# The small products of a triangular solver, given a higher priority in the schedule of a decoder layer

## The chip, the core and the metric

The kernel runs on one core of a Trainium2 chip. The metric is the device time of one execution in microseconds (us); the kernel before takes 859.18 us (median of three runs, 858.14 to 862.75).

## What is computed

One decoder layer over 512 positions of width 1024. A combined input projection feeds a pooling mixer and a gated DeltaNet mixer of 8 heads; the two are gated, added, projected, normalised, and go through a feed-forward block and an embedding gate. The change touches one step of the DeltaNet mixer alone, the unit lower triangular solve inside each chunk of 64 positions:

```python
m = jnp.where(strict, jnp.einsum('bnhid,bnhjd->bnhij', kb, k) * decay, 0.0)
a = m + jnp.eye(CHUNK, dtype=m.dtype)
rhs = jnp.concatenate([v * beta[..., None], kb * jnp.exp(gc)[..., None]], axis=-1)
sol = lax.linalg.triangular_solve(a, rhs, left_side=True, lower=True, unit_diagonal=True)
...
def step(state, inp):                      # the scan over the chunks
    v_new = u_n - jnp.einsum('bhcd,bhde->bhce', w_n, state)
    o = jnp.einsum('bhcd,bhde->bhce', qg_n, state) + jnp.einsum('bhij,bhje->bhie', attn_n, v_new)
    state = state * jnp.exp(gl_n)[..., None, None] + jnp.einsum('bhcd,bhce->bhde', kg_n, v_new)
```

## The kernel before

The large projections (`gemm_tile`, lines 66 to 68) are done as three products in the fp32r type, each with a 128x128 stationary tile and 512 columns. The small work of the mixer (transposes, the products of the scan, the solver) is in plain fp32; such a product shows as two records of TensorE in the trace.

The heads go in four pairs. For each pair the program has `front` (projections of k, q and v, convolution, the products k k^T and q k^T), then the `scan` of the pair before (lines 509 to 583: eight steps in four blocks of 128 positions, whose products are on lines 542, 543, 552, 558 and 559, and the transposes on line 580), then `solve` of the pair itself. After the last pair come the pooling branch, the last `scan`, the gate projections z, gb and ga, the output projection (wo), and a third stage (up and down projections, from line 827) whose instructions are kept in program order.

`solve` (lines 431 to 507) inverts eight 128x128 blocks per pair. VectorE first inverts the 16x16 diagonal blocks (lines 440 to 453); then the inverse is doubled to 32, 64 and 128 by two groups of products each:

- p16, line 461, and q16, line 468: 32 products each on 32x32 tiles
- p32, line 483, and q32, lines 491 and 493: 16 and 24 products on 32x32 tiles
- p64, line 502, and q64, line 506: 8 products each on 64x64 tiles

Between two groups ScalarE or VectorE copies the result out of PSUM (lines 463, 469 and 470, 486, 496 and 497, 503, 507), and the next group reads that copy. A group is called a burst below. There are six for a pair and 24 in all.

The order on each engine is not written out for these two stages. A scheduler runs the program in a simulated time: whenever an engine is free there, it takes from the instructions that are ready the one of highest priority, and by default that is the one that stands first in the program. So `scan` of the pair before stands ahead of `solve`, and the next pair's `front` stands behind it. The order so found is fixed in the instruction streams; on the chip each engine works through its stream in that order and waits on semaphores. Weight slabs are prepared with a priority raised by 300 (line 56).

Of the kernel before, what the change touches and what calls it, by code (L numbers as in the profile page):

```python
# [33 lines left out]
def layer(tc, x, p, ln_in_g, ln_in_b, w_in, pool_w, pool_scale, conv_w, a_log, dt_bias, o_norm_w,  # L34
          w_out, ln1_g, ln1_b, w_up, w_down, ple_gate_w, ple_proj_w, ln2_g, ln2_b, out):
    nc = tc.nc
    V, A, G, T = nc.vector, nc.scalar, nc.gpsimd, nc.tensor
# [107 lines left out]
    for t in range(NT):  # L145
        xt = mxp.tile([P, DM], F32, tag="big", name=f"x_{t}")
# [62 lines left out]
    for t in range(NT):  # L209
# [7 lines left out]
        a, b = xts[t][:, 0:cut], xts[t][:, cut:1024]  # L217
# [123 lines left out]
    x64, p64 = xp64[0:64], xp64[64:128]  # L341
# [89 lines left out]
    def solve(pr, n, yfull):  # L431

        U8 = 2 * NT
        w = lambda tag, shape, bufs=1: tp1.tile(list(shape), F32, tag=tag, bufs=bufs, name=f"{tag}_{pr}")
        n32 = w("p16", (P, U8, 32))
        for q in range(4):
            r = slice(32 * q, 32 * q + 32)
            A.copy(n32[r], n[r, :, r])
        b16 = w("b16", (P, U8, 16))
        V.tensor_scalar(out=b16, in0=n32[:, :, 0:16], scalar1=lowm, scalar2=None, op0=MULT)  # L440
        V.scalar_tensor_tensor(out=b16, in0=n32[:, :, 16:32], scalar=highm, in1=b16, op0=MULT, op1=ADD)
        ya = w("ya", (P, U8, 16))
        V.tensor_copy(ya, eye16.unsqueeze(1).to_broadcast([P, U8, 16]))
        for k in range(15):
            m = 15 - k
            sh = w("sh", (P, U8, 16), 2)
            V.stream_shuffle(out=sh[:, :, :m], in_=b16[:, :, k + 1:], mask=[k] * 16 + [16 + k] * 16)
            V.tensor_tensor(out=sh[:, :, :m], in0=sh[:, :, :m],
                            in1=ya[:, :, k:k + 1].to_broadcast([P, U8, m]), op=MULT)
            V.tensor_tensor(out=ya[:, :, k + 1:], in0=ya[:, :, k + 1:], in1=sh[:, :, :m], op=ADD)  # L450
        y = w("yc", (P, U8, 32))
        V.tensor_scalar(out=y[:, :, 0:16], in0=ya, scalar1=lowm, scalar2=None, op0=MULT)
        V.tensor_scalar(out=y[:, :, 16:32], in0=ya, scalar1=highm, scalar2=None, op0=MULT)
        xt = w("xc", (P, U8, 32))
        V.transpose(out=xt, in_=y)

        pp = pp1.tile([P, U8, 32], F32, tag="sp", name=f"ps_p16_{pr}")
        for u in range(U8):
            for q in range(4):
                r = slice(32 * q, 32 * q + 32)  # L460
                T.matmul(pp[r, u, :], n[r, u, r], xt[r, u, :], start=True, stop=True)
        p16 = w("p16", (P, U8, 32))
        A.copy(p16, pp)
        pq = pp1.tile([P, U8, 16], F32, tag="sq", name=f"ps_q16_{pr}")
        for u in range(U8):
            for q in range(4):
                r = slice(32 * q, 32 * q + 32)
                T.matmul(pq[r, u, :], p16[r, u, :], y[r, u, 16:32], start=True, stop=True)
        V.scalar_tensor_tensor(out=y[:, :, 16:32], in0=pq, scalar=lowm, in1=y[:, :, 16:32], op0=MULT, op1=ADD)
        V.transpose(out=xt, in_=y)  # L470
        for q in range(4):
            r = slice(32 * q, 32 * q + 32)
            A.copy(yfull[r, :, r], y[r])
        for q in range(2):
            r = slice(32 * q, 32 * q + 32)
            A.copy(x64[r, :, r], xt[r])

        pp = pp1.tile([P, U8, 32], F32, tag="sp", name=f"ps_p32_{pr}")
        p32 = w("p16", (P, U8, 32))
        for q in (0, 2):  # L480
            r, r1 = slice(32 * q, 32 * q + 32), slice(32 * q + 32, 32 * q + 64)
            for u in range(U8):
                T.matmul(pp[r1, u, :], n[r, u, r1], xt[r, u, :], start=True, stop=True)
        for q in (0, 2):
            r1 = slice(32 * q + 32, 32 * q + 64)
            A.copy(p32[r1], pp[r1])
        pq = pp1.tile([P, U8, 32], F32, tag="sq", name=f"ps_q32_{pr}")
        for q in (0, 2):
            r, r1 = slice(32 * q, 32 * q + 32), slice(32 * q + 32, 32 * q + 64)
            for u in range(U8):  # L490
                T.matmul(pq[r, u, :], p32[r1, u, :], y[r1, u, :], start=True, stop=True)
                if q == 0:
                    T.matmul(pq[r1, u, :], y[r1, u, :], p32[r1, u, :], start=True, stop=True)
        for q in (0, 2):
            r, r1 = slice(32 * q, 32 * q + 32), slice(32 * q + 32, 32 * q + 64)
            A.copy(yfull[r, :, r1], pq[r])
        A.copy(x64[32:64, :, 0:32], pq[32:64])

        a, b = slice(0, 64), slice(64, 128)
        pp = pp1.tile([P, U8, 64], F32, tag="sp", name=f"ps_p64_{pr}")  # L500
        for u in range(U8):
            T.matmul(pp[b, u, :], n[a, u, b], x64[:, u, :], start=True, stop=True)
        A.copy(p64, pp[b])
        pq = pp1.tile([P, U8, 64], F32, tag="sq", name=f"ps_q64_{pr}")
        for u in range(U8):
            T.matmul(pq[a, u, :], p64[:, u, :], yfull[b, u, b], start=True, stop=True)
        A.copy(yfull[a, :, b], pq[a])

    def scan(heads, yfull, kq, kg, vs, sm, last=False):
# [90 lines left out]
    def lazy(pr):  # L600
        got = {"k": wk0} if pr == 0 else {}

        class Groups:
            def __getitem__(self, n):
                if n not in got:
                    with tc.issue_after(vec_last.ins), tc.issue_after(act_last.ins):
                        got[n] = wslab({"k": C_K, "q": C_Q, "v": C_V}[n] + 256 * pr, f"{n}{pr}")
                return got[n]
        return Groups()

    prev = None
    for pr in range(NH // 2):
        heads, npr, yfull, kq, kg, vs, sm = front(pr, lazy(pr))
        if prev is not None:
            scan(*prev)
        solve(pr, npr, yfull)
        prev = (heads, yfull, kq, kg, vs, sm)
# [7 lines left out]
    for s in range(2):  # L625
        gr = wslab(C_POOL + 256 * s, f"pool{s}")
        for m in range(2):
# [4 lines left out]
            u = tpa.tile([P, SEQ], F32, tag="acc", bufs=2, name=f"u_{g}")  # L632
# [11 lines left out]
            n = win - 1  # L644
# [224 lines left out]
    def fetch(c, name, i, half):  # L869
        raw = wide(f"{name}_{c}").rearrange("p (j n) -> p j n", j=2)  # L870
        oS.dma_start(out=raw, in_=quarter(c, i, half))
        return raw
# [100 lines left out]
    x, z, y, b22 = fetch(0, "x", 0, 0), fetch(0, "z", 1, 0), None, None  # L973
    oS.dma_start(out=gain1, in_=ln1_g[0].partition_broadcast(P))
    oS.dma_start(out=off1, in_=ln1_b[0].partition_broadcast(P))
    y, b22 = fetch(0, "y", 0, 1), fetch(0, "w", 1, 1)
# [8 lines left out]
    for c in range(NC):  # L985
# [44 lines left out]
        if not lst:  # L1030
# [11 lines left out]
            x, z, y, b22 = nxt + [fetch(c + 1, "y", 0, 1), fetch(c + 1, "w", 1, 1)]  # L1042
# [16 lines left out]
    u = tp3.tile([P, 2, SEQ], F32, tag="r2", bufs=2, name="u")  # L1059
# [111 lines left out]
```

## Time and profile before

| | us |
|---|---|
| median of three runs | 859.18 |
| lowest, highest | 858.14, 862.75 |
| the profiled execution | 858.59 |
| its span, first to last instruction | 856.9 |
| TensorE busy | 838.3 |
| VectorE busy | 612.6 |
| ScalarE busy | 407.8 |

PE is TensorE's matmul, PEld its weight load, DVE is VectorE, ACT is ScalarE. The profiled execution takes 1.7 us more than its span, which lies around the first and the last instruction. In a timeline the first number of a line is its start, the second the time from there to the end of the last record on that line. Matmuls are pipelined and their ends are modelled, so lines overlap; the pace is read from start to start.

### The profile page before, as it was taken

The page shows a single profiled execution, that of the slowest core. Times are in us where ns is not written, and L with a number is a line of the kernel's source. Part 1 is how long each engine was busy: PE and PEld are TensorE (multiplying, and loading weights), DVE is VectorE, ACT ScalarE, POOL GpSimd, SP SyncE. Part 2 cuts the span into 40 slices and gives each one's busy share as a digit, 9 for nine tenths or more (in the row PEclk, how much of TensorE's full clock was granted, in tenths as well). Part 3 has the DMA queues.
Part 4 walks back from the last instruction along what each step waited for, and adds up shares of the span by engine and source line. Part 5 has one row for each costly group of instructions (what it writes and reads, how often), then busy time and mean ns, then how long its engine had stood idle before and what let it go on. Part 6 is the DMA issues. An engine that isn't in the chain of part 4 may idle for free.

```text
span 856.9 us, 12524 instructions
## 1 busy us (share of the span) xinstructions
PE 838.3 (98%) x4848; PEld 697.6 (81%) x4848; DVE 612.6 (71%) x1197; ACT 407.8 (48%) x648; POOL 88.1 (10%) x94
## 2 busy tenths in 40 slices
PE   7999999999999999999999999999999999999996
PEld 6787888888888888888889878888888888888785
DVE  7898968759768436469467795848575767667986
ACT  5566455465464534342309544453535453634510
POOL 4061000002001000010000101111111111110000
PEclk9999999999999999999999999999999999999999
DMA  6323322222221322246216757575757576655221
GB/s 203 98 55 94 88 61 69 81 65 59 81 75 32 86 65 80 73 138 212 100 49 208 187 148 172 126 173 138 175 139 183 135 187 146 158 139 123 75 75 49
DMA packets 73229, 98.47 MB, mean 115 GB/s; under 512 B 4553, under 2 KB 48978, under 8 KB 73170
## 3 DMA queue, kind: packets, MB, share of 16 engines
q1 hardware_dynamic: 64384, 80.87, 29.7%
q0 software_dynamic: 8704, 16.78, 12.0%
q8 instruction: 38, 0.62, 0.3%
q14 instruction: 21, 0.17, 0.1%
q10 hardware_dynamic: 82, 0.02, 0.0%
HBM read 95.56 MB, written 2.10 MB: 114 GB/s over the span
## 4 chain that ended last, share of the span: by engine, by line
PE 86%; DVE 7%; ACT 3%; DMA 2%; issue 1%; POOL 0%; DVEq 0%; SPq 0%; ACTq 0%; POOLq 0%
PE ps_up L839 18%; PE ps_pg L839 5%; PE ps_dny L839 5%; PE ps_dnx L839 5%; PE ps_dn L839 4%; PE ps_dnz L839 2%; PE ps_z L68 2%; PE ps_gb L67 2%; PE ps_z L67 2%; PE ps_ga L68 2%; PE ps_gb L68 2%; PE ps_gb L66 2%; PE ps_z L66 2%; PE ps_ga L66 2%; PE ps_ga L67 2%; DVE res L839 1%
## 5 line engine op out<-in xcount | busy, mean ns | idle before, releaser
L839 PE MATMUL ps_up<-act,hi_up 128*128 128x512 f32 x480 | 147.8, 389 | 0.0
L839 PEld LDWEIGHTS ps_up<-act,hi_up 128*128 128x128 f32 x480 | 90.0, 188 | 18.7
L839 PE MATMUL ps_up<-act,lo_up 128*128 128x512 f32 x240 | 93.4, 389 | 0.0
L839 ACT ACTIVATE r<-ps_up 128x512 f32<-128x512 f32 x32 | 19.1, 596 | 101.4 <-PE ps_up L839 99.5
L839 POOL DMA_DIRECT2D x<-in_w_down_dram x24 | 29.0, 1210 | 279.0 <-DVE lo_dn L839 266.6
L839 PEld LDWEIGHTS ps_up<-act,lo_up 128*128 128x128 f32 x240 | 45.0, 188 | 9.3
L839 DVE TENSOR_TENSOR lo_dn<-x,hi_dn 128x1024 fp32r<-128x1024 f32 x32 | 39.0, 1220 | 6.9 <-ACT hi_dn L839 6.9
L839 PE MATMUL ps_dnx<-hi_dn,hid_s 128*128 128x512 f32 x128 | 42.3, 391 | 0.0
L839 ACT CAST hid_s<-r 128x512 fp32r<-128x512 f32 x32 | 18.3, 618 | 46.1 <-DVE r L839 46.1
L839 ACT CAST hi_dn<-x 128x1024 fp32r<-128x1024 f32 x32 | 33.6, 1051 | 12.3 <-PE ps_dn L839 9.0
L839 PE MATMUL ps_pg<-hi_pg,act 128*128 128x512 f32 (+1 forms) x128 | 36.0, 362 | 0.0
L839 DVE TENSOR_TENSOR hid_b<-r,hid_b 128x512 fp32r<-128x512 f32 x16 | 11.1, 692 | 32.0 <-ACT hid_b L839 32.0
L839 DVE TENSOR_TENSOR lo_up<-raw_up,hi_up 128x1024 fp32r<-128x1024 f32 x28 | 33.5, 1218 | 0.0
L839 DVE TENSOR_TENSOR hid_a<-r,hid_a 128x256 fp32r<-128x256 f32 x16 | 6.8, 425 | 35.2 <-ACT hid_a L839 35.2
L839 DVE TENSOR_TENSOR r<-r 128x256 f32<-128x256 f32 x64 | 27.2, 425 | 2.2
L839 DVE TENSOR_TENSOR hid_s<-r,hid_s 128x512 fp32r<-128x512 f32 x32 | 20.7, 688 | 11.1 <-ACT hid_s L839 11.1
L839 ACT CAST hi_up<-raw_up 128x1024 fp32r<-128x1024 f32 x28 | 28.6, 1045 | 0.0
L839 PEld LDWEIGHTS ps_dnx<-hi_dn,hid_s 128*128 128x128 f32 x128 | 23.9, 188 | 5.7 <-DVE hid_s L839 0.4
L839 PEld LDWEIGHTS ps_pg<-hi_pg,act 128*128 128x128 f32 x128 | 23.1, 189 | 3.8
L576 POOL TENSOR_TENSOR rs<-rs,mhalf 128x4 f32<-128x4 f32 x8 | 9.4, 1174 | 162.8 <-DVE rs L575 162.8
L839 PE MATMUL ps_dnx<-lo_dn,hid_s 128*128 128x512 f32 x64 | 24.9, 389 | 0.0
L839 PE MATMUL ps_dnz<-hi_dn,hid_b 128*128 128x512 f32 x64 | 22.4, 391 | 2.1 <-DVE hid_b L839 2.1
(735 smaller groups left out, 2414.1 us busy)
## 6 DMA issues: line engine op xcount, KB each, us to landing
raw_up<-in_w_up_dram SPq DMA_DIRECT2D x32, 512.0 KB, 6.9
x<-in_w_down_dram POOLq DMA_DIRECT2D x24, 512.0 KB, 5.9
raw_wo<-in_w_out_dram SPq DMA_DIRECT2D x8, 512.0 KB, 4.5
x<-in_w_down_dram SPq DMA_DIRECT2D x8, 512.0 KB
z<-in_w_down_dram SPq DMA_DIRECT2D x8, 512.0 KB
y<-in_w_down_dram SPq DMA_DIRECT2D x8, 512.0 KB
w<-in_w_down_dram SPq DMA_DIRECT2D x8, 512.0 KB, 3.6
y<-in_w_down_dram POOLq DMA_DIRECT2D x8, 512.0 KB, 8.8
```

What stands on the lines that cost most here:

```text
L66: T.matmul(ps, wh, ah, start=first, stop=False)
L67: T.matmul(ps, wh, al, start=False, stop=False)
L68: T.matmul(ps, wl, ah, start=False, stop=last)
L576: G.tensor_tensor(out=rs, in0=rs, in1=mhalf.to_broadcast([P, NT]), op=ALU.pow)
L839: return lambda *a, **k: tc.keep_in_program_order(op(*a, **k))
```

## The change

The six groups of matmuls in `solve` are each put into a block `tc.high_priority(offset=1000)`. That raises the priority of these instructions by 1000 places, which is more than the instructions of `scan` and `front` before them, so in the scheduler's choice they stand ahead of anything else that is ready on TensorE. No instruction is added or removed, and none of the copies between the bursts is in such a block.

```diff
         pp = pp1.tile([P, U8, 32], F32, tag="sp", name=f"ps_p16_{pr}")
-        for u in range(U8):
-            for q in range(4):
-                r = slice(32 * q, 32 * q + 32)
-                T.matmul(pp[r, u, :], n[r, u, r], xt[r, u, :], start=True, stop=True)
+        with tc.high_priority(offset=1000):
+            for u in range(U8):
+                for q in range(4):
+                    r = slice(32 * q, 32 * q + 32)
+                    T.matmul(pp[r, u, :], n[r, u, r], xt[r, u, :], start=True, stop=True)
...
         pq = pp1.tile([P, U8, 32], F32, tag="sq", name=f"ps_q32_{pr}")
-        for q in (0, 2):
-            r, r1 = slice(32 * q, 32 * q + 32), slice(32 * q + 32, 32 * q + 64)
-            for u in range(U8):
-                T.matmul(pq[r, u, :], p32[r1, u, :], y[r1, u, :], start=True, stop=True)
-                if q == 0:
-                    T.matmul(pq[r1, u, :], y[r1, u, :], p32[r1, u, :], start=True, stop=True)
+        with tc.high_priority(offset=1000):
+            for q in (0, 2):
+                r, r1 = slice(32 * q, 32 * q + 32), slice(32 * q + 32, 32 * q + 64)
+                for u in range(U8):
+                    T.matmul(pq[r, u, :], p32[r1, u, :], y[r1, u, :], start=True, stop=True)
+                    if q == 0:
+                        T.matmul(pq[r1, u, :], y[r1, u, :], p32[r1, u, :], start=True, stop=True)
...
         pq = pp1.tile([P, U8, 64], F32, tag="sq", name=f"ps_q64_{pr}")
-        for u in range(U8):
-            T.matmul(pq[a, u, :], p64[:, u, :], yfull[b, u, b], start=True, stop=True)
+        with tc.high_priority(offset=1000):
+            for u in range(U8):
+                T.matmul(pq[a, u, :], p64[:, u, :], yfull[b, u, b], start=True, stop=True)
```

q16, p32 and p64 are changed in the same way.

## Rows read from the trace of the kernel before

**Rows 1.** The page: busy time of the engines, and the chain that ended last.
```profile
PE 838.3 (98%) x4848; PEld 697.6 (81%) x4848; DVE 612.6 (71%) x1197; ACT 407.8 (48%) x648; POOL 88.1 (10%) x94
...
PE 86%; DVE 7%; ACT 3%; DMA 2%; issue 1%; POOL 0%; DVEq 0%; SPq 0%; ACTq 0%; POOLq 0%
```

**Rows 2.** Busy time in three stretches: us, PE, PEld, DVE, ACT, POOL, clock, DMA.
```profile
80.00:100.00 20.00, 19.46 (x92) 15.85 (x91) 19.93 (x74) 8.23 (x12) 1.65 (x1) 1.00 0.36 105
100.00:460.00 360.00, 360.00 (x2626) 301.30 (x2625) 244.41 (x594) 164.21 (x303) 15.51 (x13) 1.00 0.28 83
460.00:500.00 40.00, 37.59 (x218) 32.70 (x217) 31.29 (x43) 24.51 (x45) 5.58 (x5) 1.00 0.75 210
```

**Rows 3.** TensorE's longest wait from 400 us on: total, times, longest.
```profile
PE ps_dnz L839 <- DVE hid_b L839: 2.1, 1, 2.1
```

**Rows 4.** TensorE's timeline: the first broken burst, q16 of the second pair.
```profile
168.64 0.61 PE L468 MATMUL ps_q<-yc,p 32*32 32x16 f32 x50
169.18 0.49 PE L558 MATMUL ps_s<-vn,kg 128*128 128x128 f32 x2
169.51 0.39 PE L559 MATMUL ps_s<-vn,E 128*128 128x128 f32 x2
169.82 0.25 PE L468 MATMUL ps_q<-yc,p 32*32 32x16 f32 x8
...
170.65 0.24 PE L468 MATMUL ps_q<-yc,p 32*32 32x16 f32 x6
170.82 0.50 PE L68 MATMUL ps_q<-act,lo_q3a 128*128 128x512 f32 x1
```

**Rows 5.** TensorE's timeline: the last broken burst, q64 of the fourth pair.
```profile
308.75 0.32 PE L506 MATMUL ps_q<-yfull,xp 64*64 64x64 f32 x2
...
311.16 0.50 PE L66 MATMUL ps_gb<-act,hi_gb1a 128*128 128x512 f32 x1
```

**Rows 6.** TensorE's timeline: four products of the scan between projections.
```profile
160.83 0.39 PE L68 MATMUL ps_k<-act,lo_k3a 128*128 128x512 f32 x1
161.06 0.38 PE L542 MATMUL ps_s<-S,kq 128*128 128x128 f32 x2
...
161.87 0.48 PE L66 MATMUL ps_k<-act,hi_k3a 128*128 128x512 f32 x1
162.19 0.39 PE L67 MATMUL ps_k<-act,hi_k3a 128*128 128x512 f32 x1
```

**Rows 7.** TensorE's timeline: two whole bursts of the first pair and what follows them.
```profile
119.25 0.73 PE L468 MATMUL ps_q<-yc,p 32*32 32x16 f32 x64
119.90 0.66 PE L358 MATMUL ps_kt<-ident,kq 128*128 128x128 f32 x4
...
139.38 1.14 PE L502 MATMUL ps_p<-xp,n 64*64 64x64 f32 x16
140.45 0.50 PE L66 MATMUL ps_v<-act,hi_v2b 128*128 128x512 f32 x1
140.79 0.39 PE L67 MATMUL ps_v<-act,hi_v2b 128*128 128x512 f32 x1
```

**Rows 8.** TensorE's timeline: a whole burst with the scan right behind it.
```profile
237.49 0.73 PE L468 MATMUL ps_q<-yc,p 32*32 32x16 f32 x64
238.15 0.49 PE L558 MATMUL ps_s<-vn,kg 128*128 128x128 f32 x2
...
238.62 0.48 PE L68 MATMUL ps_z<-act,lo_z0a 128*128 128x512 f32 x1
238.93 0.40 PE L66 MATMUL ps_z<-act,hi_z0a 128*128 128x512 f32 x1
```

**Rows 9.** Timelines of ScalarE and TensorE: last copy before q64, second pair, and q64.
```profile
192.01 0.58 ACT L503 COPY xp<-ps_p 64x512 f32<-64x512 f32 x1 [2.26 <-PE ps_p L502]
...
194.17 1.02 PE L506 MATMUL ps_q<-yfull,xp 64*64 64x64 f32 x14
```

**Rows 10.** TensorE's timeline: the first product of the output projection.
```profile
410.51 0.48 PE L754 MATMUL ps_wo<-hi_wo,mx 128*128 128x512 f32 x1
```

More of the change, by code (lines that the diff above doesn't have):

```diff
@@ L464, in solve @@
         pq = pp1.tile([P, U8, 16], F32, tag="sq", name=f"ps_q16_{pr}")
-        for u in range(U8):
-            for q in range(4):
-                r = slice(32 * q, 32 * q + 32)
-                T.matmul(pq[r, u, :], p16[r, u, :], y[r, u, 16:32], start=True, stop=True)
+        with tc.high_priority(offset=1000):
+            for u in range(U8):
+                for q in range(4):
+                    r = slice(32 * q, 32 * q + 32)
+                    T.matmul(pq[r, u, :], p16[r, u, :], y[r, u, 16:32], start=True, stop=True)
         V.scalar_tensor_tensor(out=y[:, :, 16:32], in0=pq, scalar=lowm, in1=y[:, :, 16:32], op0=MULT, op1=ADD)
@@ L479, in solve @@
         p32 = w("p16", (P, U8, 32))
-        for q in (0, 2):
-            r, r1 = slice(32 * q, 32 * q + 32), slice(32 * q + 32, 32 * q + 64)
-            for u in range(U8):
-                T.matmul(pp[r1, u, :], n[r, u, r1], xt[r, u, :], start=True, stop=True)
+        with tc.high_priority(offset=1000):
+            for q in (0, 2):
+                r, r1 = slice(32 * q, 32 * q + 32), slice(32 * q + 32, 32 * q + 64)
+                for u in range(U8):
+                    T.matmul(pp[r1, u, :], n[r, u, r1], xt[r, u, :], start=True, stop=True)
         for q in (0, 2):
@@ L487, in solve @@
         pq = pp1.tile([P, U8, 32], F32, tag="sq", name=f"ps_q32_{pr}")
-        for q in (0, 2):
-            r, r1 = slice(32 * q, 32 * q + 32), slice(32 * q + 32, 32 * q + 64)
-            for u in range(U8):
-                T.matmul(pq[r, u, :], p32[r1, u, :], y[r1, u, :], start=True, stop=True)
-                if q == 0:
-                    T.matmul(pq[r1, u, :], y[r1, u, :], p32[r1, u, :], start=True, stop=True)
+        with tc.high_priority(offset=1000):
+            for q in (0, 2):
+                r, r1 = slice(32 * q, 32 * q + 32), slice(32 * q + 32, 32 * q + 64)
+                for u in range(U8):
+                    T.matmul(pq[r, u, :], p32[r1, u, :], y[r1, u, :], start=True, stop=True)
+                    if q == 0:
+                        T.matmul(pq[r1, u, :], y[r1, u, :], p32[r1, u, :], start=True, stop=True)
         for q in (0, 2):
@@ L500, in solve @@
         pp = pp1.tile([P, U8, 64], F32, tag="sp", name=f"ps_p64_{pr}")
-        for u in range(U8):
-            T.matmul(pp[b, u, :], n[a, u, b], x64[:, u, :], start=True, stop=True)
+        with tc.high_priority(offset=1000):
+            for u in range(U8):
+                T.matmul(pp[b, u, :], n[a, u, b], x64[:, u, :], start=True, stop=True)
         A.copy(p64, pp[b])
         pq = pp1.tile([P, U8, 64], F32, tag="sq", name=f"ps_q64_{pr}")
-        for u in range(U8):
-            T.matmul(pq[a, u, :], p64[:, u, :], yfull[b, u, b], start=True, stop=True)
+        with tc.high_priority(offset=1000):
+            for u in range(U8):
+                T.matmul(pq[a, u, :], p64[:, u, :], yfull[b, u, b], start=True, stop=True)
         A.copy(yfull[a, :, b], pq[a])
```

## The prediction

> **What bounds the kernel now.** I read the page first: TensorE is busy 98% of the span, and 86% of the chain that ended last is TensorE's [rows 1]. Then the table by stretches: from 100 to 460 us, which holds all 24 bursts of the solver, the scans and the gate and output projections, TensorE has no idle time at all, at full clock, while VectorE works 244 of 360 us and ScalarE 164 [rows 2]. So in this stage only TensorE's own work counts. A wait of VectorE or ScalarE there costs nothing, and every microsecond that TensorE saves is a microsecond earlier at 460 us. Behind it TensorE waits a little, at most 2.1 us at once [rows 3]. Last I read TensorE's timeline from 110 to 315 us line by line, for what a burst costs and where it is cut.
>
> **What stands there.** All six bursts of the first pair are whole; no scan runs beside them. Of the 18 bursts of the other three pairs ten are cut: in the second pair q16 and q32 into three pieces each, p64 and q64 into two; in the third p16 into three and p32 into two; in the fourth p16 and p32 into two, q32 and q64 into three. Those are 25 pieces, so 15 breaks; the first and the last of the ten are shown [rows 4, 5]. What stands in a break is always a product or transpose of the scan, never a projection. That fits the program: scan stands ahead of solve, everything else that is ready stands behind it. A burst of higher priority than the scan should therefore come out whole.
>
> **What a break costs.** I read prices from start to start.
> - A product of the scan among projections: the four in [rows 6] take 161.06 to 161.87, 0.81 us, and the first projection product behind them takes 0.32 us (161.87 to 162.19) in place of the usual 0.23 (160.83 to 161.06). Together 0.90, or 0.225 us each.
> - A whole burst: q16 takes 0.65 us, p64 1.07 us [rows 7]; q64 has the same count and shape as p64.
> - The cut q16 of the second pair takes 168.64 to 170.82, 2.18 us, with four scan products in its two breaks [rows 4]. Whole it would be 0.65 + 4 x 0.225 = 1.55. So two breaks cost 0.63, 0.315 each.
> - The cut q64 of the fourth pair takes 308.75 to 311.16, 2.41 us, with three scan products in its two breaks [rows 5]. Whole: 1.07 + 3 x 0.225 = 1.745. Two breaks cost 0.665, 0.33 each.
>
> The price hardly depends on the kind of burst: a break is one more change of TensorE from the small tiles to 128x128 and back. I take 0.325, the middle of the two.
>
> Does the price go away when the scan's products move behind the burst, or only move with them? A whole burst with two scan products right behind shows it [rows 8]: the products take 238.15 to 238.62, 0.47, and the next projection product 0.31; less two products at 0.225, 0.33 is left for that first projection product. Directly behind a whole burst the first projection product takes 0.34 as well (140.45 to 140.79 [rows 7]). So a scan group behind a whole burst costs nothing extra, and the full price is saved.
>
> **The sum.** 15 breaks x 0.325 = 4.9 us less work on TensorE. 858.6 - 4.9 = 853.7 us, against the profiled execution (span 856.9 and 1.7 around it). That execution lies 0.6 us under the median of the runs; from the median the same sum gives 854.3.
>
> **What moves.** The bursts come earlier by at most the scan products that they overtake; TensorE takes its stream in order, so a burst whose operand isn't there would stop everything behind it. The copies that feed the bursts end well before: I compared each of the 24 starts with the end of the copy before it. The least distance is q64 of the second pair, 1.58 us (copy ends 192.59, burst starts 194.17 [rows 9]); the others have 3.3 us or more. A burst overtakes rarely more than four products, 0.9 us. So I cost the new waits at nothing; the cover is the 1.6 us, and if it were gone the price would be the lack, burst by burst. The scan's products come later by at most the rest of a burst, 1.07 us [rows 7]. Behind them wait VectorE and ScalarE, which have about a third of their time and more free here [rows 2], and in the end the gating of the heads, far later in the stage. No DMA and no instruction of SyncE or GpSimd is in the raised blocks; weight slabs follow TensorE's releases and are ready several microseconds ahead, so they shift with it.
>
> A rule of the Trainium skill speaks for a smaller gain. The rows show 0.315 to 0.33 us for a break [rows 4, 5]. "TensorEngine Tiling (Array Packing)", section "Tiling Modes", says that changing the tiling mode drains the engine, and "TensorE: Matmul & The Clock Gate", section "Step-by-step: what each phase is for", puts a drain at 128 cycles. An estimate from these pages is two drains of 53 ns at 2.4 GHz, 0.11 us for a break, and 1.6 us in all, which would give 857.0 us. The trace shows three times as much for a break, and the sum goes by the trace (rival 1 has a like time, worked out from rows).
>
> **The rivals.**
> 1. *Only the short pieces' own overhead is saved*, because what the scan pays beside a burst it pays elsewhere too. The last piece of q16 takes 0.17 us for 6 records [rows 4]; at the whole burst's 0.65 / 64 = 0.010 per record that leaves 0.11 for a break, 15 x 0.11 = 1.7 us, 856.9 us. Against it stand [rows 8], where the scan behind a whole burst pays no more. Chance 0.09.
> 2. *The saving is given back behind 460 us.* There TensorE is idle 2.4 of 40 us and VectorE busy 31 [rows 2], and its longest wait there, 2.1 us, is for VectorE [rows 3]. If VectorE's backlog did not move with TensorE, half to all of the 4.9 us would turn into such waits: 856.1 to 858.6 us. Against it: what VectorE does there is set free by TensorE's own results, so the stage should shift as a whole. Chance 0.15.
> 3. *The bursts are not quite whole.* q32 reads two copies (line 486), one for each half; with top priority its first half could be taken at once and the second later, with projections between. Four such bursts at 0.325 are 1.3 us: 855.0 us. Against it: q32 of the first pair is whole with projections ready beside it. Chance 0.08.
> 4. *Slower: TensorE waits at the raised bursts.* If the scheduler, in its simulated time, put each of the 18 bursts of pairs two to four one ScalarE copy too early (0.58 us [rows 9]), that is 10.4 us of waits in a stage without any: 858.6 - 4.9 + 10.4 = 864.1 us. It decides from 0.27 us of wait for each burst on (4.9 / 18). For it: the order of the whole stage after the second pair is found anew, and where VectorE was full, at 80 to 100 us, TensorE did idle 0.5 of 20 us [rows 2]. Against it: the distance of 1.6 us and more. Chance 0.07.
> 5. *More is saved*, by a new order that happens to put bursts side by side without a change of tile between them: two or three meetings at 0.33, 852.5 us or less. Chance 0.05.
>
> **How the numbers follow.** My forecast, 853.7 us, has the rest, 0.56; its own range is 852 to 855.5, from the prices 0.315 and 0.333 (4.7 to 5.0 us) and the spread of the runs. The range of 8 in 10 reaches from 851.5 to 858.4: it takes in rivals 1 to 3 but for a gain lost completely, and leaves out the slower one. 0.5%, about what a measurement of this kernel can tell from no change, is 4.3 us; the forecast lies only 0.6 us beyond it. So of its 0.56 I count 0.46 as faster, with rival 5 and a share of rival 3 that makes 0.55. The rest of these with rivals 1 and 2 is within 0.5%, 0.38. Slower by over 0.5% is rival 4, 0.07.
>
> **What would show it.** Right: 24 whole bursts in TensorE's timeline, q16 still at 0.65 us and p64 at 1.07, the scan's products in groups behind them, no idle time from 100 to 460 us, the output projection starting some 5 us earlier than at 410.5 us [rows 10], and the wait of [rows 3] as long as it was. Rival 1: the first four of these, but a start of the output projection only 1.7 us earlier. Rival 2: that start 5 us earlier, and longer waits after 460 us. Rival 3: q32 in two pieces with projections between. Rival 4: idle time of TensorE in front of lines 461 to 506, released by ScalarE or VectorE. The prediction would be wrong, too, if the new order moved other work between the stages, so that counts of records between 100 and 460 us differ.

## The result, and the profile of the changed kernel

The changed kernel takes 855.36 us (median of 12 runs, 854.03 to 857.33); the kernel before takes 860.10 us in the 12 runs measured beside it. The ratio is 0.9948, with a 95% interval of 0.9939 to 0.9957: 0.5% faster, 4.7 us by the medians. The profiled execution of the changed kernel takes 855.31 us, its span 853.6.

The page of the changed kernel, its busy times and the shares of the chain that ended last; against [rows 1] TensorE is 4.9 us less busy, VectorE as busy as it was:

```profile
PE 833.4 (98%) x4848; PEld 695.2 (81%) x4848; DVE 612.6 (72%) x1197; ACT 407.0 (48%) x648; POOL 86.6 (10%) x94
...
PE 86%; DVE 7%; ACT 4%; DMA 2%; issue 1%; POOL 0%; SPq 0%; DVEq 0%; ACTq 0%; POOLq 0%
```

TensorE's timeline of the changed kernel at the two bursts that stood cut in [rows 4] and [rows 5]:

```profile
167.79 0.39 PE L558 MATMUL ps_s<-rr,yfull 128*128 128x128 f32 x2
168.10 0.73 PE L470 MATMUL ps_q<-yc,p 32*32 32x16 f32 x64
168.76 0.49 PE L558 MATMUL ps_s<-rr,yfull 128*128 128x128 f32 x2
169.09 0.39 PE L564 MATMUL ps_s<-vn,kg 128*128 128x128 f32 x2
169.31 0.39 PE L565 MATMUL ps_s<-vn,E 128*128 128x128 f32 x2
169.45 0.49 PE L68 MATMUL ps_q<-act,lo_q3a 128*128 128x512 f32 x1
...
302.25 1.14 PE L512 MATMUL ps_q<-yfull,xp 64*64 64x64 f32 x16
303.32 0.49 PE L564 MATMUL ps_s<-vn,kg 128*128 128x128 f32 x2
```

Both are whole: q16 takes 0.66 us from start to start, q64 1.07, and the scan's products stand behind them. All 24 bursts are whole; there is no break left.

To see where the gain arises and where it goes, I cut the span at four places: the first burst (p16 of the first pair), the transposes ps_pT ahead of the output projection, its first product, and the first product of the up projection. In the changed kernel they are these:

```profile
113.57 0.75 PE L462 MATMUL ps_p<-xc,n 32*32 32x32 f32 x64
...
404.61 1.03 PE L743 MATMUL ps_pT<-ident,ptok 128*128 128x128 f32 x8
406.17 0.50 PE L760 MATMUL ps_wo<-hi_wo,mx 128*128 128x512 f32 x1 [0.53 <-ACT sga L716]
...
464.52 0.48 PE L912 MATMUL ps_up<-act,hi_up 128*128 128x256 f32 x2
```

In the kernel before the first product of the output projection stands at 410.51 us [rows 10], and the other three here:

```profile
113.88 0.75 PE L461 MATMUL ps_p<-xc,n 32*32 32x32 f32 x64
...
409.72 1.03 PE L737 MATMUL ps_pT<-ident,ptok 128*128 128x128 f32 x8
...
469.03 0.48 PE L906 MATMUL ps_up<-act,hi_up 128*128 128x256 f32 x2
```

| stretch | before, us | after, us | gain, us |
|---|---|---|---|
| start to first burst | 113.88 | 113.57 | 0.31 |
| first burst to ps_pT | 295.84 | 291.04 | 4.80 |
| ps_pT to output projection | 0.79 | 1.56 | -0.77 |
| output projection to up projection | 58.52 | 58.35 | 0.17 |
| up projection to the end | 387.85 | 389.08 | -1.23 |
| span | 856.88 | 853.60 | 3.28 |

The first line lies ahead of anything that was changed. If all of the 4.80 us are the fifteen breaks, that is 0.32 us each; the experiments test it. Two things take some of it back in this execution. One is the wait of 0.53 us in front of the output projection (line 760), which makes that stretch 0.77 us longer from start to start. The other lies in the third stage, whose stream of instructions is the same in both kernels. TensorE's waits of the changed kernel from 400 us on (total, times, longest), and its timeline at the longest, which answers to [rows 3]:

```profile
PE ps_dnz L845 <- DVE hid_b L845: 2.2, 1, 2.2
PE ps_rt L845 <- DVE res L845: 1.4, 1, 1.4
PE ps_wo L760 <- ACT sga L716: 0.5, 1, 0.5
```

```profile
491.93 0.39 PE L845 MATMUL ps_dnz<-lo_dn,hid_b 128*128 128x512 f32 x1
494.54 1.22 PE L845 MATMUL ps_dnz<-hi_dn,hid_b 128*128 128x512 f32 x2 [2.21 <-DVE hid_b L845]
495.55 0.63 PE L845 MATMUL ps_dnz<-lo_dn,hid_b 128*128 128x512 f32 x1
495.98 0.63 PE L845 MATMUL ps_dnz<-hi_dn,hid_b 128*128 128x512 f32 x1
496.41 0.63 PE L845 MATMUL ps_dnx<-hi_dn,hid_s 128*128 128x512 f32 x1
...
498.05 0.40 PE L845 MATMUL ps_dnx<-lo_dn,hid_s 128*128 128x512 f32 x1
```

The wait is as long as before. But behind it the products take 0.63 us in place of 0.39, and start 0.43 us apart in place of 0.23: the granted clock is 0.51 from 495 to 498 us and 0.70 on average from 495 to 500 us, as these stretches of the changed kernel show (columns as in [rows 2]):

```profile
495.00:498.00 3.00, 3.00 (x8) 2.32 (x8) 2.25 (x5) 1.65 (x3) 0.00 (x0) 0.51 0.99 167
495.00:500.00 5.00, 5.00 (x17) 3.93 (x17) 4.07 (x7) 3.65 (x5) 0.00 (x0) 0.70 1.03 220
```

That is the 1.23 us of the last stretch. It does not go with the change: the same fall stands behind the same wait in the profiles of the first, third, fourth (both kernels), fifth and seventh experiment, and it is missing in those of the second and the sixth and in the profiled execution of the kernel before. All of them have the same instructions there. What decides whether the clock falls at that wait is not shown.

### The profile page after: what moved, and what is told of

Read it like the earlier page. It is cut to its first block, busy times and chain, and to the rows that moved or that the text cites. A ratio compares the mean times of both kernels' runs of the same rounds, so it can differ in the third digit from the quotient of the medians.

```text
span 853.6 us, 12510 instructions
## 1 busy us (share of the span) xinstructions
PE 833.4 (98%) x4848; PEld 695.2 (81%) x4848; DVE 612.6 (72%) x1197; ACT 407.0 (48%) x648; POOL 86.6 (10%) x94
## 4 chain that ended last, share of the span: by engine, by line
PE 86%; DVE 7%; ACT 4%; DMA 2%; issue 1%; POOL 0%; SPq 0%; DVEq 0%; ACTq 0%; POOLq 0%
PE ps_up L845 18%; PE ps_pg L845 5%; PE ps_dny L845 5%; PE ps_dnx L845 5%; PE ps_dn L845 4%; PE ps_dnz L845 2%; PE ps_z L67 2%; PE ps_gb L66 2%; PE ps_z L68 2%; PE ps_z L66 2%; PE ps_gb L68 2%; PE ps_gb L67 2%; PE ps_ga L67 2%; PE ps_ga L66 2%; PE ps_ga L68 2%; DVE res L845 2%
## 5 line engine op out<-in xcount | busy, mean ns | idle before, releaser
L845 DVE TENSOR_TENSOR res<-ps_dnx,res 128x512 f32<-128x512 f32 x32 | 21.1, 686 | 5.6 <-PE ps_dnx L845 5.6
```

The lines of the kernel that those rows point to most:

```text
L845: return lambda *a, **k: tc.keep_in_program_order(op(*a, **k))
```

## The experiments

Three theories stood against each other. A: each break costs some 0.32 us of TensorE wherever it stands, and the gain is the fifteen breaks. B: only some 0.11 us is saved for a break, the short piece's own overhead (rival 1) or a drain. C: the breaks are free, and the gain comes from the new order as such. The orders are fixed when a kernel is built, so the breaks of each could be counted in its instruction stream before it ran.

**1 and 2. The price of a break, with the same work.** One extra fp32 product with a 128x128 stationary tile is put into each of 16 bursts, at the head (first run) or in the middle (second run). It has 128 columns, in q16 64; the text below calls all of them 128x128.

```diff
         with tc.high_priority(offset=1000):
             for u in range(U8):
+                if u == 0:          # second run: u == 4
+                    T.matmul(pp[:, 4:6, :], ident, xp64[:, 0:2, :], start=True, stop=True)
                 T.matmul(pp[b, u, :], n[a, u, b], x64[:, u, :], start=True, stop=True)
```

Shown is p64; p16, q16 and q64 have the like.

> The changed kernel with one extra 128x128 fp32 product at the head of each p16, q16, p64 and q64 burst, 16 in all; its result is overwritten by the burst. No burst is cut. It is the base for the next run. Every theory: 16 x 0.225 = 3.6 us more than the changed kernel, some 859.0 us; the bursts behind it as long as before (q16 0.65, p64 1.07 us).

> The same 16 extra products, but each in the middle of its burst, so that 16 of the 24 bursts are cut once by work of the same size. Theory A (a break costs 0.325 us wherever it stands): 16 x 0.325 = 5.2 us more than with the products at the head, some 864.2 us. Theory B (only the drain, or the short piece's own overhead, 0.11 us): 1.8 us more, 860.8 us. Theory C (breaks cost nothing, the gain comes from the new order as such): no difference, 859.0 us.

Measured: 860.05 us with the product at the head (ratio to the kernel before 0.9991, interval 0.9982 to 1.0000) and 863.03 in the middle (1.0037, 1.0024 to 1.0050). The ratios differ by 0.46%, 4.0 us, the medians by 3.0; A's size was 5.2, B's 1.8, C's none. The first run missed the 859.0 expected of it by 1.1 us. The stretch from the first burst to ps_pT takes 295.32 and 299.16 us, 3.84 more. In the first of these kernels it holds a wait that the second doesn't have: a product of the last tile of the gate sgb starts late, behind the sigmoid of line 706. TensorE's timeline of the first:

```profile
391.90 0.39 PE L68 MATMUL ps_gb<-act,lo_gb3b 128*128 128x512 f32 x1
392.97 0.50 PE L66 MATMUL ps_gb<-act,hi_gb3a 128*128 128x512 f32 x1 [0.69 <-ACT sgb L706]
393.31 0.40 PE L67 MATMUL ps_gb<-act,hi_gb3a 128*128 128x512 f32 x1
```

These two steps, 1.07 and 0.34 us, are 0.23 each otherwise, so 0.95 us are lost there, which is most of that miss. (Like the wait of experiments 5 and 6 it is for the sigmoid of a gate; whether it is for a bank is not shown.) Without it 16 breaks cost 4.8 us, 0.30 each. Counted burst by burst in the two traces, where a burst has the same neighbours in both, a break costs 0.28 us in p16 and q16 (32x32 tiles) and 0.33 in p64 and q64 (64x64). TensorE's timeline of both kernels at the first p64 shows one of them, first with the product at the head:

```profile
139.81 0.39 PE L68 MATMUL ps_v<-act,lo_v2b 128*128 128x512 f32 x1
140.03 0.38 PE L512 MATMUL ps_p<-xp,ident 128*128 128x128 f32 x2
140.35 1.14 PE L513 MATMUL ps_p<-xp,n 64*64 64x64 f32 x16
141.42 0.50 PE L66 MATMUL ps_v<-act,hi_v2b 128*128 128x512 f32 x1
```

and with the product in the middle:

```profile
140.36 0.39 PE L68 MATMUL ps_v<-act,lo_v2b 128*128 128x512 f32 x1
140.68 0.68 PE L513 MATMUL ps_p<-xp,n 64*64 64x64 f32 x8
141.28 0.49 PE L512 MATMUL ps_p<-xp,ident 128*128 128x128 f32 x2
141.70 0.68 PE L513 MATMUL ps_p<-xp,n 64*64 64x64 f32 x8
142.31 0.50 PE L66 MATMUL ps_v<-act,hi_v2b 128*128 128x512 f32 x1
```

From the projection product ahead of it to the one behind, the burst with its extra product takes 1.61 us uncut (139.81 to 141.42) and 1.95 cut (140.36 to 142.31): 0.34 us for this break. B and C fall. What a break is made of, a drain, a weight load or something else, these runs do not show.

**3. Nine breaks fewer.** The raised priority for two pairs alone.

```diff
-        with tc.high_priority(offset=1000):
+        with tc.high_priority(offset=1000) if pr >= 2 else nullcontext():
```

> The raised priority for the bursts of the third and fourth pair alone; the second pair keeps its six breaks, so 6 of the 15 are left. Theory A: 9 breaks gone, 9 x 0.325 = 2.9 us under the kernel before, 857.2 us. Theory B: a break is worth 0.11 us, so at most 1.0 us of the gain can come from nine of them, and the rest is the order's. Theory C: the time need not lie between the two kernels.

Measured: 857.19 us, ratio 0.9964 (0.9952 to 0.9977), 3.1 us under the kernel before. The time lies between the two kernels and where A has it.

**4. The scan raised in place of the solver, and one pair alone.** One execution each, with the stretch from the first burst to ps_pT as the measure. In the first, each product of `scan` stands in `tc.high_priority(offset=1000)`, and none of `solve`. In the second:

```diff
-        with tc.high_priority(offset=1000):
+        with tc.high_priority(offset=1000) if pr == 1 else nullcontext():
```

> The kernel before, with the raised priority on the scan's products in place of the solver's. The order of the stage is a new one, but the bursts are still cut: 14 breaks in place of 15. Theory A: the time from the first p16 to the transposes ahead of the output projection falls by one break, 295.8 - 0.3 = 295.5 us. Theory C (a new order with these small products raised is what helps): it falls toward the 291.0 us of the changed kernel.

> The raised priority for the bursts of the second pair alone. Its six breaks go, but in the order that follows the third and fourth pair have 12 breaks in place of 9, so 12 of 15 are left. Theory A: the same stretch takes 295.8 - 3 x 0.32 = 294.9 us. If raising a pair's bursts were worth something by itself, without regard to breaks, it would give a third of the gain, 294.2 us or less.

The two executions took 859.85 and 860.93 us, so the whole time shows no gain: in both the clock had fallen behind the wait for hid_b, and the output projection holds a wait of 0.5 and 0.8 us that the kernel before does not have. The stretch ends ahead of these.

With the runs above this gives a row of five kernels of the same work and other orders; the last column is 291.04 + 0.32 for each break, so its first and last rows fit by construction and the three between them are the test:

| kernel | breaks | first burst to ps_pT, us | 0.32 a break, us |
|---|---|---|---|
| before | 15 | 295.84 | 295.84 |
| scan raised | 14 | 295.38 | 295.52 |
| second pair alone | 12 | 294.95 | 294.88 |
| third and fourth pair | 6 | 292.87 | 292.96 |
| changed | 0 | 291.04 | 291.04 |

No kernel is off the line by more than 0.14 us. How far the stretch varies by itself, the kernels of experiments 5 and 7 and the first of experiment 8 show: they have the same order of TensorE's products in it and take 287.77 to 288.01 us. So the row with one break fewer tells little, those with three and nine fewer tell more. Raising the second pair's bursts took away its six breaks and let three new ones arise in the later pairs, and the stretch followed the count, not the pairs raised. Together with experiments 1 and 2, the number of breaks is what the change works by.

**5. The wait in front of the output projection.** It is the part of the gain that went. My first guess was the PSUM bank that the last gate's sigmoid still reads; this run took the first block of the contraction in another order of the position blocks. It stands on top of experiment 7's kernel, which has the same wait.

```diff
-            for t in range(NT):
+            for t in ((2, 3, 0, 1) if kb == 0 else range(NT)):
                 ah, al = lhs(kb, 0, t), lhs(kb, 1, t)
```

> The kernel with the tiles side by side, and in the output projection the first block of the contraction taken for the position blocks 2, 3, 0, 1 in place of 0, 1, 2, 3. If the new wait of 0.8 us in front of the output projection is for the PSUM bank that the last gate's sigmoid (line 716) still reads, the first product now goes to another bank and the wait is gone: 0.8 us less than with the tiles side by side alone, 852.2 us. If it is for the operands (weights or mixed activations), the wait stays: 853.0 us.

Measured: 852.50 us, ratio 0.9910 (0.9895 to 0.9926), and the stretch from ps_pT to the first product is still 1.56 us. The expectation missed. But it did not tell the two causes apart: in the built program the tile which is used first gets bank 0, whichever position block it is for.

**6. The last gate tile in another bank.**

```diff
-            ps = gps(f"ps_ga{o}")
+            ps = pp1.tile([P, SEQ], F32, tag="sp", bufs=1, name="ps_ga7") if o == 7 else gps(f"ps_ga{o}")
```

> The kernel with the tiles side by side, and the last gate tile (ps_ga of block 7, line 713 of the changed kernel) put into the PSUM bank that the solver's bursts used, in place of one of the two that the projections take in turn. In the built programs the first product of the output projection always goes to bank 0, whichever position block it is for (that is why the reordered blocks of the run before met the same wait); the last gate tile stands in bank 1 in the kernel before and in bank 0 in the changed one. If that is the wait of 0.8 us, it goes now: 0.8 us less than 853.0, 852.2 us, and the stretch from the transposes to the first product is 0.79 us again in place of 1.56. If the wait is for an operand, it stays at 1.56.

Measured: 851.28 us, ratio 0.9902 (0.9887 to 0.9918). TensorE's timeline of this kernel at the same place:

```profile
402.62 1.03 PE L743 MATMUL ps_pT<-ident,ptok 128*128 128x128 f32 x8
403.41 0.48 PE L760 MATMUL ps_wo<-hi_wo,mx 128*128 128x512 f32 x1
```

From 402.62 to 403.41 it is 0.79 us, as in the kernel before, and the wait is gone. The whole time could not show this: the interval overlaps with that of experiment 7's kernel. So it was the bank. The projections take two banks in turn. The first product of the output projection goes to bank 0 in both kernels; the last gate tile is in bank 1 in the kernel before and in bank 0 with the new order, so the product waits for the sigmoid that reads it. In the changed kernel's ScalarE timeline that sigmoid stands behind a cast:

```profile
404.57 1.05 ACT L57 CAST hi_wo<-raw_wo 128x1024 fp32r<-128x1024 f32 x1 [1.49 <-PE ps_ga L67]
405.52 0.59 ACT L716 ACTIVATE sga<-ps_ga 128x512 f32<-128x512 f32 x1
```

It ends at 406.11, and the product starts at 406.17. In the kernel before the sigmoid stands behind the same cast, and in this experiment's kernel too:

```profile
410.64 0.59 ACT L710 ACTIVATE sga<-ps_ga 128x512 f32<-128x512 f32 x1
```

```profile
402.87 0.59 ACT L716 ACTIVATE sga<-ps_ga 128x512 f32<-128x512 f32 x1
```

There the first product does not wait for it: it starts at 410.51, ahead of the sigmoid, and at 403.41, before the sigmoid's end at 403.46.

**7. What a whole burst still costs.** p32 and q32 take 1.02 and 1.03 us, p16 with twice the products 0.68. In the changed kernel the loops over the blocks and over the two halves are exchanged, for q32 in the same way:

```diff
-            for q in (0, 2):
-                r, r1 = slice(32 * q, 32 * q + 32), slice(32 * q + 32, 32 * q + 64)
-                for u in range(U8):
+            for u in range(U8):
+                for q in (0, 2):
+                    r, r1 = slice(32 * q, 32 * q + 32), slice(32 * q + 32, 32 * q + 64)
                     T.matmul(pp[r1, u, :], n[r, u, r1], xt[r, u, :], start=True, stop=True)
```

> The changed kernel with the loops of p32 and q32 exchanged: for each block both halves q=0 and q=2, in place of all blocks of q=0 and then all of q=2. Same products, other order inside the burst. If a burst's length is set by the products on its busiest 32x32 tile (8 x 0.065 us and 0.12 us of entry and exit), p32 goes from 1.02 to 0.64 us and q32 from 1.03 to 0.65, 8 x 0.38 = 3.0 us less: 852.3 us. If two tiles don't run side by side, nothing changes: 855.4 us.

Measured: 853.01 us, ratio 0.9918 (0.9904 to 0.9931); the stretch falls from 291.04 to 287.85 us, 3.2 us. TensorE's timeline at p32 of the first pair, in the kernel before (as long in the changed one) and in this one:

```profile
125.95 1.09 PE L483 MATMUL ps_p<-xc,n 32*32 32x32 f32 x32
126.97 0.33 PE L358 MATMUL ps_kt<-ident,kq 128*128 128x128 f32 x1
```

```profile
126.05 0.69 PE L486 MATMUL ps_p<-xc,n 32*32 32x32 f32 x32
126.68 0.55 PE L358 MATMUL ps_kt<-ident,kq 128*128 128x128 f32 x3
```

1.02 us has become 0.63: 16 products, alternating between two tiles, take about as long as the 32 of p16 on four. So products on different 32x32 tiles run side by side here if they alternate in the stream; eight in a row on one tile do not.

**8. The wait for hid_b, and a kernel faster than both.** Two kernels move the scaling of the residual in the first block of the third stage, whose work on VectorE delays hid_b. The first puts it later (on top of experiment 5), the second earlier (on top of experiment 6), into a gap of VectorE. The diff is that of the second.

```diff
+        if fst:
+            alpha_h(1)
         w[5] = split_dn(x, f"{c}5")
         onto(x, c, 1, 1)
...
-        if fst:
-            alpha_h(1)
         left[0] = odd_block(c, 0, ps, r2, ha)
```

> On top of that, in the first block of the third stage, the scaling of the residual of position blocks 2 and 3 (lines 1021 and 1026 of the changed kernel) is put behind the second odd block, and behind the gather of z, so that VectorE gets to hid_b sooner. TensorE's wait of 2.2 us for hid_b should be gone; with it the halved clock that followed it in some executions, where four TensorE products in a row took 0.63 in place of 0.39 us. Expected 2.2 us from the wait and about 1.2 us more wherever the clock had fallen: 848.8 to 850.0 us. If VectorE's backlog only moves to the next product, the wait comes back there: 852 us.

> On top of that, the scaling of the residual of position block 1 (line 1018 of the changed kernel) is put ahead of the split of the accumulated weights for product 5, where VectorE sits idle for 3.3 us until a transfer has landed. VectorE's work behind it then comes 2.4 us earlier, hid_b among it. Expected: TensorE's wait of 2.1 us for hid_b goes, and with it the stretch of halved clock behind it, where one fell: 2.1 to 3.3 us, 849.0 to 850.1 us. If VectorE's backlog is the bound as a whole, the wait comes back at a later product, as it did when that work was put later: 852 us.

Later: 852.73 us (0.9923, 0.9910 to 0.9936), nothing gained over 852.50. TensorE's waits from 400 us on show that the wait for hid_b only moved:

```profile
PE ps_dnx L845 <- DVE res L845: 1.8, 1, 1.8
PE ps_rt L845 <- DVE res L845: 1.4, 1, 1.4
PE ps_dny L845 <- DVE res L845: 1.3, 2, 0.9
```

Earlier: 848.76 us (0.9870, 0.9855 to 0.9885), 2.5 us under experiment 6, and the same list has:

```profile
PE ps_rt L845 <- DVE res L845: 1.4, 1, 1.4
PE ps_up L912 <- DVE act L124: 0.3, 1, 0.3
PE ps_dnz L845 <- DVE hid_b L845: 0.3, 1, 0.3
```

The wait is 0.3 in place of 2.1 us, and in the profiles, neither of which has the fallen clock there, the stretch from the up projection on takes 386.04 in place of 387.84 us: 1.8 of the 2.5 us are the wait. This kernel, with whole bursts, side by side tiles, the last gate in its own bank and the work in the gap, is 1.3% faster than the kernel before.

## Why the prediction was right, and where it was off

**The breaks and their count: right.** Fifteen breaks by the scan alone, none left after the change. The price of 0.325 us is the term of the sum that carried everything, and the stretch that holds the bursts gives 4.80 / 15 = 0.32; the row of five kernels agrees for other counts. That it hardly depends on the kind of burst holds roughly: experiments 1 and 2 give 0.28 on 32x32 tiles and 0.33 on 64x64.

**That the price goes away and does not only move: right.** It was read from one place, [rows 8]. Experiments 1 and 2 show it with the same work on both sides, 0.30 a break. Rival 1 is out. The estimate of 0.11 us from the pages of the Trainium skill that stood beside it ("TensorEngine Tiling (Array Packing)", section "Tiling Modes", with the 128 cycles of "TensorE: Matmul & The Clock Gate", section "Step-by-step: what each phase is for") is about a third of what a break costs here; no run shows how long the drain itself takes.

**No waits at the raised bursts: right.** In the changed kernel no burst has idle time of TensorE's matmuls ahead of it, so rival 4's mechanism did not set in. Rival 3 neither: q32 is whole.

**No idle time from 100 to 460 us: wrong in one place.** TensorE waits 0.53 us ahead of the output projection, and that costs 0.77 us from start to start. Two steps of the prediction missed it: "So I cost the new waits at nothing", which was reasoned from the operands of the bursts alone, and the sentence that a wait of VectorE or ScalarE in this stage costs nothing. The order of the stage was found anew, and with it the bank of the last gate tile changed; then one sigmoid of ScalarE held TensorE up. Rival 2 expected the gain to be given back, but behind 460 us and by VectorE, and half of it or more. I had looked at when operands are ready, not at which bank a tile lands in. The output projection also runs past the 460 us within which the prediction has it, to 469.03 us; nothing hangs on that.

**The base: the larger part of the miss.** The forecast of 853.7 us is 1.7 us under the 855.36 measured. The sum was made against the profiled execution, 858.59 us. In 12 runs the kernel before has a median of 860.10; the profiled one is among its fastest, and it did not have the fallen clock behind the wait for hid_b, which costs 1.2 us where it falls. From 860.10 the same 4.9 us give 855.2. The gain by the medians, 4.7 us, is close to the forecast 4.9, but partly by luck. The traces give 4.80 less 0.77, 4.0 us, for the stages that the change touches. And in the executions whose granted clock is the highest on average, 0.998, the changed kernel takes 854.03 and 854.44 us and the kernel before, in the runs measured beside the experiments, 857.97 to 858.61 (six): 4.0 us apart by the middle values. The rest of the 4.7 would then lie in how often the clock fell in the executions of each kernel, which is argued and not shown. The interval of the ratio (0.43 to 0.61%, 3.7 to 5.2 us) leaves room for both, and it holds the 0.5% beyond which the prediction put a chance of 0.55.

## What to carry to other kernels

Where small tiles of TensorE run among full ones, count the changes between them in the instruction stream: on a TensorE that never waits, each one that a burst is cut by was paid in full here, and a burst kept whole and with its products alternating between the tiles cost the least. When a scheduler finds an order anew, look at what changes far from the edit, above all which PSUM bank the next stage's first tile gets. And take as the base of a sum the median of several runs, or know what sets the profiled execution apart from it.

## What the runs showed of the hardware

- A break of a burst, one more change from 32x32 or 64x64 tiles to 128x128 and back, costs 0.28 us on 32x32 and 0.33 on 64x64 tiles with fp32 products (experiments 1 and 2, burst by burst), 0.32 over the fifteen of this change.
- Products on different 32x32 tiles overlap, and a burst's length goes by the products on one tile: 16 products on two tiles take 1.02 us in blocks of eight and 0.63 alternating, 32 alternating on four tiles 0.68.
- After a wait of 2.2 us on VectorE, TensorE's products started 0.43 us apart in place of 0.23, at a granted clock of 0.51 of full speed, the lower of the two levels (1.2 in place of 2.4 GHz). In other executions the same wait had no such effect. Where it fell it cost 1.2 us: the third stage from the up projection on took 389.08 us with it and 387.85 without.
- A product that is first to write a PSUM bank waited for ScalarE's reader of that bank, 0.53 us (0.77 from start to start); with the reader's tile in another bank the wait was gone.
